# Projections of a transformer layer: SP's loads and VectorE's operations in source order, weight loads and splits by step, q statistics by pairs of tiles

## The chip, the core and the metric

The kernel runs on one core of a Trainium2 chip. The core has TensorE (PE, matmuls, with PEld for its weight loads), VectorE (DVE), ScalarE (ACT), GpSimd (POOL) and SyncE (SP, which here only issues DMAs). The metric is device time in microseconds of one execution; lower is better. Times of the kernel before are given as the median of three runs.

## The reference

One layer over 1,024 latent tokens of width 1,024 with 256 context tokens, all in float32. The part that matters here is the projection of the modulated input to queries, keys, values and gates:

```python
mod = jax.nn.silu(c) @ w_mod[l] + b_mod[l]            # 6 x 1024 modulation columns
h_c = ctx * (1.0 + mods_c[1]) + mods_c[0]             # context, modulated
kv_ctx = _context_kv(h_c, w_in[l], b_in[l], k_norm_g[l])
h = x * (1.0 + scale1) + shift1
proj = h @ w_in + b_in                                # q_a, k_a, v_a, q_b, k_b, v_b, gates
q_a = _rope_2d(heads(OFF_QA, OFF_KA, A_HEADS), rope)
q_b = _rope_2d(_qk_rms(heads(OFF_QB, OFF_KB, B_HEADS), q_norm_g), rope)
k_b = _rope_2d(_qk_rms(heads(OFF_KB, OFF_VB, B_KV_HEADS), k_norm_g), rope)
```

`_qk_rms` divides each head by the root of its mean square; `_rope_2d` is the axial rotation. After it come windowed attention (branch a, 8 heads) and global attention (branch b, 8 heads), the merge of both through sigmoid gates, a layer norm, a SwiGLU ConvFFN with 2,816 channels and a second layer norm. The output must be exact to float32's order, so each product is made of three matmuls.

## The kernel before

**Number format.** Every operand of a large product is split into a rounded high part and a low rest (`split`, line 81): ACT (or GpSimd) casts, and VectorE or GpSimd subtracts. `mm3` (line 90) issues high x high (L91), then the second operand's low part (L92), then the first operand's low part (L93).

**Order of the work.** The framework's planner orders each engine's instructions: it takes the program's order as priority and runs what it believes ready. Only from line 1192 on is PE's order that of the source. In the stage of this change, the projections, the planner orders all engines.

**Stages.** First the eight k steps of branch b's queries (`q1acc`, eight tiles of 128 tokens), each with its weights and two modulation columns. Their evacuation (`q_evac`, line 308) adds the bias. Then a list `order` (line 707) of groups runs: 3 gates, qa (tiles 0 to 3 of branch a's queries, eight k steps of 12 matmuls), 4 gates, qb (tiles 4 to 7, the same), 4 gates, ka (keys and values of tiles 0 to 4, eight k steps of 15), 1 gate, kb (tiles 5 to 7 and the two context tiles 8 and 9, steps of 15, six of them with context operands), 4 gates. A gate is one column tile of 128 channels in two halves of 512 tokens, 24 matmuls each.

**Weights.** `prefetch` (line 632) loads a weight into one of three `raw` buffers through SP's queue and splits it into `wp` buffers, eight in all, so four pairs. For gates GpSimd makes the low part (`wlg`), for q and kv weights VectorE (`wlqa`, `wlqb`, `wlka`, `wlkb`). For kb it also loads context (`cx`), modulates it on ACT and splits it on VectorE (`ch`, `cl`). The loop calls `prefetch` as far ahead as eight buffers allow: `ahead = [2 if gi in (0, 2, 3) else 4 for gi, _ in order]`, `while nxt < len(order) and sum(ahead[n:nxt + 1]) <= 8`.

**Modulation columns.** 48 columns (512 KB each) that are not needed at the start are handed out by `mods` (line 659), in proportion to the matmuls issued up to the last k step of ka. Each is a load on SP into a rotating 4 KB slot (`tmp`, from the list `hfree`) and one multiply-and-reduce on VectorE (L191).

**Side work.** `side_step` (line 696) runs one step of every post in flight and takes a new post from `queue`, each second time while `slow` is set. Posts are `qpost` (branch b: s1 with a folded rotation table on GpSimd and the statistics through `rms_scale`, s2 with the rotation; branch a: the rotation alone) and `kv_post` (s1: value split, statistics, rotation of branch a's key; s2: scaling, rotation and split of the keys; s3: four transposes on PE and copies). One rotation in three goes to GpSimd, the others to VectorE. The statistics of q square a tile on ACT into one half of `sqq`, reduce it on VectorE (L300), scale it there (L301), take the power on GpSimd (L302) and negate there (L337). At the last k step of ka and kb the sums are evacuated at once (L744) into one of two `kv` tiles. PSUM has eight banks, which accumulators, gates and transposes share.

Of the kernel before, what the change touches and what calls it, by code (L numbers as in the profile page):

```python
# [65 lines left out]
WARM = 5, 12  # L66
DNS = {u0 + 2 * n + (u0 == 20): (n, j0, j1) for u0, j0, j1 in ((16, 0, 4), (20, 4, 8), (24, 8, 11)) for n in range(3)}
# [3 lines left out]
def layer_kernel(  # L71
# [44 lines left out]
    mhalf = ctile([P, 8], F32, "mhalf")  # L116
# [179 lines left out]
    def rms_scale(x3, H, nm, sq, ss=None):  # L296
        nc.scalar.activation(sq.rearrange("p (h d) -> p h d", d=HD), x3, AF.Square)
        if ss is None:
            ss = ph1.tile([P, 8], F32, tag="ss", name=f"ss{nm}", bufs=4)[:, 0:H]
# [21 lines left out]
    def qpost(br, t):  # L321
# [36 lines left out]
    def kv_post(t, kv):  # L358
        st = {}
        kb = kv[:, 128:256].rearrange("p (h d) -> p h d", d=HD)  # L360

        def s1():
            vt = VT[t // 2][:, t % 2]
# [11 lines left out]
        def s2():  # L375
            rms_apply(kb, 2, st["ss"])
# [255 lines left out]
    def prefetch(gi, k):  # L632
        if gi == "g":
            hs = []
            for a in (0, 1):
                wr = raw(f"wg{k}_{a}")
                nc.sync.dma_start(wr.rearrange("p (a b) -> p a b", b=P), w_g[k][:, 4 * a:4 * a + 4])
                hs.append(wsplit(wr, f"g{k}_{a}", "gpsimd"))
            ready[gi, k] = hs
            return  # L640
        nm, src, tiles = groups[gi]
        wr = raw(f"w{nm}{k}")
        nc.sync.dma_start(wr, src[k])
# [109 lines left out]
    while queue or flight:  # L753
        side_step()
# [997 lines left out]
```

## Time and profile before

| what | value |
|---|---|
| median of 3 runs | 1588.32 us (1586.73 to 1589.17) |
| profiled execution | 1587.44 us |
| its span, first to last instruction | 1585.7 us |
| granted clock of PE, mean | 0.992 |
| PE busy | 1537.8 us (97%) |
| VectorE busy | 1195.1 us (75%) |
| ACT busy | 812.8 us (51%) |
| GpSimd busy | 753.0 us (47%) |

The projections behind branch b's queries take from about 55 to 344 us of the span. Busy time counts an instruction from its start to its end; matmuls overlap, each shown with some 0.39 us while the next starts 0.23 us after it, so PE's progress is best read from starts. A row of groups gives line, engine, operation, what is written from what, shapes and count, then busy us, mean ns of one, then idle time of the engine just before and what ended it. A row in order of time gives start and length in us and, in brackets, the idle time before and its releaser.

### The profile page before, as it was taken

What the parts mean: (1) busy time and instruction counts of PE and PEld (TensorE: products, weight loads), DVE (VectorE), ACT (ScalarE), POOL (GpSimd) and SP (SyncE); (2) the same over time, 40 slices, a digit from 0 to 9 for tenths busy, and PEclk for the clock granted to TensorE, in tenths of its full rate; (3) what the DMA queues carried; (4) which work ended last, traced back from release to release, by engine and by line L of the source; (5) the groups of instructions that cost most, each with busy time, mean ns of one, the idle gap of its engine ahead of it and who ended that gap; (6) DMA issues with size and microseconds to landing.
All of it is one profiled execution on the core that took longest, in us unless ns stands there. A gap on an engine that the chain in (4) does not pass through costs nothing.

```text
span 1585.7 us, 22137 instructions
## 1 busy us (share of the span) xinstructions
PE 1537.8 (97%) x7718; PEld 1275.6 (80%) x7718; DVE 1195.1 (75%) x1766; ACT 812.8 (51%) x1444; POOL 753.0 (47%) x731
## 2 busy tenths in 40 slices
PE   9999999999999999999999999999999999999996
PEld 7877788878886887777788898888888888888876
DVE  7897645628888777788674779888887887657886
ACT  5412222448888667788431565444444444435542
POOL 0673312416667556665423554666666674021132
PEclk9999999999999999999999999999999999999998
DMA  9785662322236555531451132333334446996721
GB/s 378 252 273 173 223 211 90 115 85 65 65 94 167 137 127 138 134 68 38 143 179 59 61 100 86 114 107 111 115 106 117 111 115 184 350 285 208 256 94 53
DMA packets 112225, 229.46 MB, mean 145 GB/s; under 512 B 12945, under 2 KB 27793, under 8 KB 112018
## 3 DMA queue, kind: packets, MB, share of 16 engines
q1 hardware_dynamic: 96816, 198.93, 37.9%
q0 software_dynamic: 10400, 20.19, 8.2%
q10 hardware_dynamic: 4898, 8.94, 1.5%
q8 instruction: 60, 0.98, 0.3%
q14 instruction: 51, 0.42, 0.1%
HBM read 176.83 MB, written 65.86 MB: 153 GB/s over the span
## 4 chain that ended last, share of the span: by engine, by line
PE 83%; DVE 6%; ACT 3%; issue 3%; DMA 2%; POOL 2%; ACTq 0%; SPq 0%; DVEq 0%; POOLq 0%
PE ptr L546 5%; PE p L92 4%; PE p L93 4%; PE p L91 4%; PE g L93 3%; PE g L91 3%; PE g L92 3%; PE b L93 3%; PE b L92 3%; PE b L91 3%; PE s L429 2%; PE av L567 2%; PE c L91 2%; PE d L93 2%; PE c L93 2%
## 5 line engine op out<-in xcount | busy, mean ns | idle before, releaser
L556 DVE TENSOR_TENSOR ptl<-ptr,pth 128x512 fp32r<-128x512 f32 x188 | 124.6, 684 | 27.9 <-ACT pth L555 25.6
L555 ACT CAST pth<-ptr 128x512 fp32r<-128x512 f32 x188 | 106.6, 588 | 56.6 <-PE ptr L546 32.8
L546 PE MATMUL ptr<-ident,p 128*128 128x128 f32 x816 | 126.8, 278 | 8.6 <-DVE ptl L556 6.6
L88 DVE TENSOR_TENSOR ld<-rd,hd 128x1024 fp32r<-128x1024 f32 x77 | 94.0, 1239 | 53.3 <-ACT hd L83 49.6
L441 ACT ACTIVATE p<-p,nm 128x1024 f32<-128x1024 f32 (+2 forms) x128 | 125.3, 981 | 10.6 <-DVE p L474 9.9
L546 PEld LDWEIGHTS ptr<-ident,p 128*128 128x128 f32 x816 | 93.7, 140 | 38.7 <-DVE ptl L556 12.5
L83 ACT CAST hd<-rd 128x1024 fp32r<-128x1024 f32 x77 | 79.2, 1050 | 80.4 <-PE p L93 47.1
L567 PE MATMUL av<-pth,VT 128*128 128x512 f32 x236 | 104.6, 443 | 1.0 <-ACT avs L573 0.5
L91 PE MATMUL p<-hd 128*128 128x512 f32 x264 | 103.2, 391 | 0.0
L93 PE MATMUL p<-hd,ld 128*128 128x512 f32 x264 | 102.7, 389 | 0.0
L92 PE MATMUL p<-ld,hd 128*128 128x512 f32 x264 | 102.7, 389 | 0.0
L93 PE MATMUL g<-hh,wlg 128*128 128x512 f32 x256 | 99.9, 390 | 0.9 <-POOL wlg L88 0.8
L91 PE MATMUL g<-hh,whg 128*128 128x512 f32 x256 | 100.0, 391 | 0.6 <-ACT whg L83 0.6
L88 POOL TENSOR_TENSOR wlg<-wg,whg 128x512 fp32r<-128x512 f32 x32 | 48.3, 1518 | 108.5 <-ACT whg L83 107.6
L92 PE MATMUL g<-hl,whg 128*128 128x512 f32 x256 | 99.6, 389 | 0.0
L568 PE MATMUL av<-ptl,VT 128*128 128x512 f32 x236 | 97.6, 414 | 2.0 <-POOL ptl L88 1.8
L474 DVE TENSOR_SCALAR_CACHE_REDUCE p<-s,cvt,nmc 128x1024 f32<-128x1024 f32 x64 | 84.4, 1339 | 12.3 <-PE s L430 12.0
L429 PE MATMUL s<-KL,q 128*128 128x512 f32 (+2 forms) x192 | 76.0, 396 | 3.8 <-ACT p_x L441 2.0
L191 DVE CUSTOM_DVE_ANT_0 wml<-wml,sc,bmc 128x1024 f32<-128x1024 f32 x32 | 44.5, 1399 | 39.3 <-DMA wml<-in_wmodT_dram 38.8
L85 POOL TENSOR_SCALAR pth<-prw 128x512 fp32r<-128x512 f32 x48 | 31.4, 653 | 86.1 <-ACT prw L552 62.0
L83 ACT CAST wS<-s 128x512 fp32r<-128x512 f32 x76 | 45.3, 621 | 51.8 <-POOL s L1094 51.0
L430 PE MATMUL s<-KL,q 128*128 128x512 f32 (+2 forms) x192 | 71.7, 373 | 0.0
(402 smaller groups left out, 4981.4 us busy)
## 6 DMA issues: line engine op xcount, KB each, us to landing
wml<-in_wmodT_dram SPq DMA_DIRECT2D x48, 512.0 KB
ru<-in_w_up_dram SPq DMA_DIRECT2D x38, 512.0 KB
rd<-td SPq DMA_DIRECT2D x55, 256.0 KB
rd<-sd SPq DMA_DIRECT2D x44, 256.0 KB
rd<-in_w_dn_dram SPq DMA_DIRECT2D x33, 256.0 KB
wm<-in_wmodT_dram SPq DMA_DIRECT2D x16, 512.0 KB
wg<-in_w_g_dram SPq DMA_DIRECT2D x32, 256.0 KB
sgd<-sg ACTq DMA_DIRECT2D x32, 256.0 KB
```

The lines of the kernel that those rows point to most:

```text
L83: nc.scalar.copy(hi, src)
L88: lo_eng.tensor_tensor(out=lo, in0=src, in1=hi.bitcast(F32), op=ALU.subtract)
L91: nc.tensor.matmul(ps, a[0], b[0], start=start, stop=False, skip_group_check=resumed)
L92: nc.tensor.matmul(ps, a[0], b[1], start=False, stop=False, skip_group_check=resumed)
L93: nc.tensor.matmul(ps, a[1], b[0], start=False, stop=stop, skip_group_check=resumed)
L429: nc.tensor.matmul(o, self.q[0][:, hs], ks, start=True, stop=False)
L441: nc.scalar.activation(p, s, AF.Exp, bias=nm[:, h:h + 1], scale=scale, accum_out=sm[:, h:h + 1])
L546: nc.tensor.transpose(tr[:, h * P:(h + 1) * P], self.pslice(h, n), ident)
L555: nc.scalar.copy(hi, tr)
L556: nc.vector.tensor_tensor(out=lo, in0=tr, in1=hi.bitcast(F32), op=ALU.subtract)
L567: nc.tensor.matmul(self.av, v, hi, start=first, stop=False)
L568: nc.tensor.matmul(self.av, v, lo, start=False, stop=self.left == 0)
```

## The change

1. The whole list runs in a region in which VectorE and SP issue in the source's order (`manual_schedule`); PE, ACT and GpSimd stay with the planner, and so does the place of the region's instructions among earlier and later ones of VectorE and SP.
2. The list is cut into steps (a gate half or a k step). At step n the load of step n+5 is issued (`WLOAD`), then the split of step n+3 (`WSPLIT`), then the context load of step n+2 and the context split of step n+1, for steps of both kv groups.
3. Columns are loaded four ahead (`MLOAD`); each `mods` call works on one that was loaded earlier and loads the next.
4. The statistics of q cover two tiles: one square of 128x1024, one reduction, one scale, one power, one negation. The squares of tiles 0 to 3 are issued among the evacuations, later ones right behind the reduction of four tiles before; `sqq` has two slots for it.
5. The evacuation of a kv tile moves from the end of its group into the post's s1.
6. Once all columns are done, a gate half is followed by two side steps.

```diff
-    def rms_scale(x3, H, nm, sq, ss=None):
+    def rms_scale(x3, H, nm, sq):
         nc.scalar.activation(sq.rearrange("p (h d) -> p h d", d=HD), x3, AF.Square)
-        if ss is None:
-            ss = ph1.tile([P, 8], F32, tag="ss", name=f"ss{nm}", bufs=4)[:, 0:H]
+        ss = ph1.tile([P, 8], F32, tag="ss", name=f"ss{nm}", bufs=4)[:, 0:H]
         nc.vector.tensor_reduce(out=ss, in_=sq.rearrange("p (h d) -> p h d", d=HD), axis=AX.X, op=ALU.add)
@@ -330,21 +332,37 @@
         def s1():
             st["tb"] = ph1.tile([P, 2, HD], F32, tag="tb", name=f"tbq{t}", bufs=4)
             gfold(st["tb"], 0, t, nc.gpsimd)
-            rms_scale(q3, 8, f"q{t}", sqq[0][:, t % 2], pqs[:, t])
-            if t == NT - 1:
-                sqq.clear()
-                hput("sqq")
-            nc.gpsimd.tensor_scalar(out=nqs[:, t], in0=pqs[:, t], scalar1=-1.0, scalar2=0.0, op0=ALU.mult, op1=ALU.add)
...
+            if t % 2 == 0:
+                qstats(t)
 
...
-    sqq = [ht("sqq", (P, 2, 512))]
+    sqq = [ht(f"sqq{n}", (P, 2, 512)) for n in (0, 1)]
+
+    def qsquare(t):
+        nc.scalar.activation(sqq[t // 2 % 2].rearrange("p a b -> p (a b)"), Q[1, t].rearrange("p a b -> p (a b)"),
+                             AF.Square)
+
+    def qstats(t):
+        sq = sqq[t // 2 % 2]
+        ss, ns = (a[:, t:t + 2].rearrange("p a b -> p (a b)") for a in (pqs, nqs))
+        nc.vector.tensor_reduce(out=ss, in_=sq.rearrange("p a (h d) -> p (a h) d", d=HD), axis=AX.X, op=ALU.add)
+        if t + 4 < NT:
+            qsquare(t + 4)
+        nc.vector.tensor_scalar(out=ss, in0=ss, scalar1=1.0 / HD, scalar2=QK_EPS, op0=ALU.mult, op1=ALU.add)
+        nc.gpsimd.tensor_tensor(out=ss, in0=ss, in1=mhalf, op=ALU.pow)
+        nc.gpsimd.tensor_scalar(out=ns, in0=ss, scalar1=-1.0, scalar2=0.0, op0=ALU.mult, op1=ALU.add)
+        if t + 2 == NT:
+            hput("sqq0", "sqq1")
+
     bias_qb = bias_tile(b_qb, "bias_qb")
     for t in range(NT):
         q_evac(1, t, acc[t], bias_qb)
+        if t in (1, 3):
+            qsquare(t - 1)
 
...
-    def kv_post(t, kv):
+    def kv_post(t, acc):
         st = {}
-        kb = kv[:, 128:256].rearrange("p (h d) -> p h d", d=HD)
 
         def s1():
+            kv = st["kv"] = ph1.tile([P, 512], F32, tag="kv", name=f"kv{t}", bufs=KVB)
+            nc.vector.tensor_tensor(out=kv, in0=acc, in1=bias_kv, op=ALU.add)
+            kb = st["kb"] = kv[:, 128:256].rearrange("p (h d) -> p h d", d=HD)
             vt = VT[t // 2][:, t % 2]
             v3 = kv[:, 256:512].rearrange("p (h d) -> p h d", d=HD)
             nc.scalar.copy(vt[:, :, 0:HD], v3)
...
-    def prefetch(gi, k):
+    def wload1(gi, k, a):
         if gi == "g":
-            hs = []
-            for a in (0, 1):
-                wr = raw(f"wg{k}_{a}")
-                nc.sync.dma_start(wr.rearrange("p (a b) -> p a b", b=P), w_g[k][:, 4 * a:4 * a + 4])
-                hs.append(wsplit(wr, f"g{k}_{a}", "gpsimd"))
-            ready[gi, k] = hs
-            return
-        nm, src, tiles = groups[gi]
-        wr = raw(f"w{nm}{k}")
-        nc.sync.dma_start(wr, src[k])
-        c = None
-        if NT in tiles:
-            cx = ph1.tile([P, NC], F32, tag="cx", name=f"cx{k}", bufs=2)
-            nc.sync.dma_start(cx, ctxT[k])
-            nc.scalar.activation(cx, cx, AF.Identity, bias=modx[:, k:k + 1], scale=modx[:, 8 + k:9 + k])
-            c = [ph1.tile([P, NC], R32, tag="ch", name=f"c{a}{k}", bufs=4) for a in "hl"]
-            split(cx, *c, nc.vector, nc.vector)
-        ready[gi, k] = wsplit(wr, f"{nm}{k}"), c
+            wr = raw(f"wg{k}_{a}")
+            nc.sync.dma_start(wr.rearrange("p (a b) -> p a b", b=P), w_g[k][:, 4 * a:4 * a + 4])
+        else:
+            wr = raw(f"w{groups[gi][0]}{k}")
+            nc.sync.dma_start(wr, groups[gi][1][k])
+        ready[gi, k, a, "raw"] = wr
+
+    def wpair(gi, k, a):
+        wr = ready.pop((gi, k, a, "raw"))
+        if gi == "g":
+            ready[gi, k, a] = wsplit(wr, f"g{k}_{a}", "gpsimd")
+        else:
+            ready[gi, k, a] = wsplit(wr, f"{groups[gi][0]}{k}")
+
+    def cload(gi, k):
+        cx = ready["cx", k] = ph1.tile([P, NC], F32, tag="cx", name=f"cx{k}", bufs=2)
+        nc.sync.dma_start(cx, ctxT[k])
+
+    def cpair(gi, k):
+        cx = ready.pop(("cx", k))
+        nc.scalar.activation(cx, cx, AF.Identity, bias=modx[:, k:k + 1], scale=modx[:, 8 + k:9 + k])
+        c = ready["c", k] = [ph1.tile([P, NC], R32, tag="ch", name=f"c{a}{k}", bufs=4) for a in "hl"]
+        split(cx, *c, nc.vector, nc.vector)
 
     late = [(col, scc, modx[:, col:col + 1]) for col in range(16)]
     late += [(col, sc, modc[:, col:col + 1]) for col in range(16, 48)]
 
     total = len(late)
     span = [0.0, 0.0]
+    coming = []
+
+    def mload():
+        col, row, o = late.pop(0)
+        w = tmp(f"wml{len(late)}")
+        nc.sync.dma_start(w, wmodT[col])
+        coming.append((col, row, o, w))
 
     def mods(us):
         span[0] += us
-        n = total - len(late)
-        for _ in range(min(int(total * span[0] / span[1] + 0.01) - n, len(late))):
-            col, row, o = late.pop(0)
-            w = tmp(f"wml{len(late)}")
-            nc.sync.dma_start(w, wmodT[col])
+        n = total - len(late) - len(coming)
+        for _ in range(min(int(total * span[0] / span[1] + 0.01) - n, total - n)):
+            col, row, o, w = coming.pop(0)
             mod(w, row, bmc[:, col:col + 1], o)
-            if not late:
+            if late:
+                mload()
+            elif not coming:
...
-        if late:
+        if late or coming:
             sg = ht(f"sg{f}_{hf}", (P, HALF))
             hput(f"sg{f}_{hf}")
...
-    ahead = [2 if gi in (0, 2, 3) else 4 for gi, _ in order]
     span[1] = sum(6 * KT if gi == "g" else 3 * len(groups[gi][2])
                   for gi, _ in order[:order.index((0, KT - 1)) + 1])
-    nxt = 0
-    for n, (gi, k) in enumerate(order):
-        while nxt < len(order) and sum(ahead[n:nxt + 1]) <= 8:
-            prefetch(*order[nxt])
-            nxt += 1
+    steps = [(gi, k, a) for gi, k in order for a in ((0, 1) if gi == "g" else (0,))]
+
+    def at(n, fn, *only):
+        if n < len(steps) and (not only or steps[n][0] in only):
+            gi, k, a = steps[n]
+            fn(*((gi, k) if only else (gi, k, a)))
+
+    inorder = ExitStack()
+    inorder.enter_context(tc.manual_schedule(engines={mybir.EngineType.DVE, mybir.EngineType.SP}))
+    for n in range(WLOAD):
+        at(n, wload1)
+        if n + WSPLIT - WLOAD >= 0:
+            at(n + WSPLIT - WLOAD, wpair)
+    for _ in range(MLOAD):
+        mload()
+    for n, (gi, k, a) in enumerate(steps):
+        at(n + WLOAD, wload1)
+        at(n + WSPLIT, wpair)
+        at(n + 2, cload, 0, 1)
+        at(n + 1, cpair, 0, 1)
         if gi == "g":
-            for hf in (0, 1):
-                last = gate(k, hf)
-                mods(3 * KT)
+            last = gate(k, a)
+            mods(3 * KT)
+            side_step()
+            if not (late or coming):
                 side_step()
             continue
         nm, src, tiles = groups[gi]
         if k == 0:
             acc = {t: acc_tile(f"acc{nm}{t}") for t in tiles}
             slow[0] = gi > 1
-        w, c = ready.pop((gi, k))
+        w = ready.pop((gi, k, 0))
+        c = ready.pop(("c", k), None)
         for t in tiles:
...
         mods(3 * len(tiles))
         if k == KT - 1:
             for t in tiles:
                 if gi < 2:
-                    kv = ph1.tile([P, 512], F32, tag="kv", name=f"kv{t}", bufs=KVB)
-                    nc.vector.tensor_tensor(out=kv, in0=acc[t], in1=bias_kv, op=ALU.add)
-                    queue.append(kv_post(t, kv))
+                    queue.append(kv_post(t, acc[t]))
                 else:
                     q_evac(0, t, acc[t], bias_qa)
                     queue.append(qpost(0, t))
@@ -750,6 +797,7 @@
                 queue += [[lambda u=u: units[u].qprep(acc_tile)] for u in (0, 1)]
         else:
             side_step()
+    inorder.close()
```

More of the change, by code (lines that the diff above doesn't have):

```diff
@@ L66 @@
 WARM = 5, 12
+WLOAD = 5
+WSPLIT = 3
+MLOAD = 4
 DNS = {u0 + 2 * n + (u0 == 20): (n, j0, j1) for u0, j0, j1 in ((16, 0, 4), (20, 4, 8), (24, 8, 11)) for n in range(3)}
@@ L115, in layer_kernel @@
     onesf = ctile([P, P], F32, "onesf")
-    mhalf = ctile([P, 8], F32, "mhalf")
+    mhalf = ctile([P, 16], F32, "mhalf")
     nc.vector.memset(onec, 1.0)
@@ L375, in s2 @@
         def s2():
+            kv, kb = st["kv"], st["kb"]
             rms_apply(kb, 2, st["ss"])
@@ L674, in gate @@
         for k in range(KT):
-            h, l = ready["g", f][k // 4]
+            h, l = ready["g", f, k // 4]
             n = slice(k % 4 * P, (k % 4 + 1) * P)
             mm3(ps, (h[:, n], l[:, n]), (hT[k][0][:, s], hT[k][1][:, s]), k == 0, k == KT - 1)
-        if late:
+        if late or coming:
             sg = ht(f"sg{f}_{hf}", (P, HALF))
@@ L733, in layer_kernel @@
                 s = slice(t * P, (t + 1) * P)
-                a = hT[k][0][:, s], hT[k][1][:, s]
+                x = hT[k][0][:, s], hT[k][1][:, s]
             else:
                 s = slice((t - NT) * P, (t - NT + 1) * P)
-                a = c[0][:, s], c[1][:, s]
-            mm3(acc[t], a, w, k == 0, k == KT - 1)
+                x = c[0][:, s], c[1][:, s]
+            mm3(acc[t], x, w, k == 0, k == KT - 1)
         mods(3 * len(tiles))
```

## The prediction

> **What bounds the kernel now.** I read the page first, then the stretch table, then the waits of PE, then the order of time of PE, ACT, DVE and SP around PE's longest wait.
>
> ```profile
> span 1585.7 us, 22137 instructions
> PE 1537.8 (97%) x7718; PEld 1275.6 (80%) x7718; DVE 1195.1 (75%) x1766; ACT 812.8 (51%) x1444; POOL 753.0 (47%) x731
> ```
>
> PE is the bound: it is without work for about 48 us in the whole span. A change to loads and to VectorE's order can win only what PE loses in the projections (55 to 344 us) and lose only what PE would newly wait there. So the question is where PE waits in that stage, and which wait the change would put there.
>
> ```profile
> PE accqa L92 <- DVE wlqa L88: 3.9, 1, 3.9
> PE accqb L92 <- DVE wlqb L88: 2.5, 2, 2.0
> PE g L93 <- POOL wlg L88: 0.8, 1, 0.8
> PE g L91 <- ACT whg L83: 0.6, 1, 0.6
> ```
>
> This is the whole answer of the waits for PE from 40 to 345 us (waiter, releaser, us in total, times, longest): every wait is for a split weight, and the large ones for the low half that VectorE makes (wlqa, wlqb). The order of time (start, length, instruction, idle before) gives their price; its first row is for later.
>
> ```profile
> 14.73 1.52 PE L93 MATMUL q1acc<-whqb,hl 128*128 128x512 f32 x6
> ...
> 92.62 0.39 PE L92 MATMUL accqa<-wlqa,hh 128*128 128x512 f32 x1
> ...
> 93.76 0.39 PE L91 MATMUL accqa<-whqa,hh 128*128 128x512 f32 x1
> 98.08 0.80 PE L92 MATMUL accqa<-wlqa,hh 128*128 128x512 f32 x1 [3.93 <-DVE wlqa L88]
> 98.67 0.63 PE L93 MATMUL accqa<-whqa,hl 128*128 128x512 f32 x1
> ...
> 102.94 0.47 PE L91 MATMUL accqa<-whqa,hh 128*128 128x512 f32 x1
> ...
> 176.91 0.39 PE L91 MATMUL accqb<-whqb,hh 128*128 128x512 f32 x1
> 179.33 0.50 PE L92 MATMUL accqb<-wlqb,hh 128*128 128x512 f32 x1 [2.03 <-DVE wlqb L88]
> 179.67 0.40 PE L93 MATMUL accqb<-whqb,hl 128*128 128x512 f32 x1
> 179.91 0.39 PE L91 MATMUL accqb<-whqb,hh 128*128 128x512 f32 x1
> ```
>
> Undisturbed matmuls start 0.228 us apart (five in 92.62 to 93.76). So the wait of L92 in accqa costs 98.08 - 93.76 - 0.23 = 4.1 us, and after it the eleven starts to 102.94 take 4.86 us where 2.5 would do: 2.4 us of slow clock. The wait at 179.33 costs 2.2 us, and nothing after it (starts 0.24 apart). The stretch table has the same (columns: length, then busy us of PE, PEld, DVE, ACT, POOL, granted clock, DMA share, GB/s):
>
> ```profile
> 90.00:100.00 10.00, 6.07 (x24) 4.64 (x23) 10.00 (x15) 2.87 (x5) 9.56 (x8) 0.81 0.81 280
> 100.00:110.00 10.00, 10.00 (x39) 8.11 (x38) 9.23 (x18) 1.86 (x3) 3.49 (x3) 0.84 0.87 294
> 170.00:180.00 10.00, 7.50 (x32) 5.57 (x31) 7.28 (x12) 1.86 (x3) 0.00 (x0) 1.00 0.71 271
> ```
>
> Why is wlqa late?
>
> ```profile
> 92.32 0.63 ACT L297 ACTIVATE sqq<-Q 128x512 f32<-128x512 f32 x1 [6.86 <-DVE cvt L300]
> 92.86 1.12 ACT L83 CAST whqa<-wqa 128x512 fp32r<-128x512 f32 x2
> ...
> 94.53 1.83 DVE L191 CUSTOM_DVE_ANT_0 wml<-wml,scc,bmc 128x1024 f32<-128x1024 f32 x1
> 96.29 1.73 DVE L88 TENSOR_TENSOR wlqa<-wqa,whqa 128x512 fp32r<-128x512 f32 x1
> ...
> 85.20 11.51 SPq L665 DMA_DIRECT2D wml<-in_wmodT_dram  x5
> 98.05 0.33 SPq L643 DMA_DIRECT2D wqa<-in_w_qa_dram  x1
> ```
>
> Three lines of work meet. ACT stood 6.9 us before a square of q, which waited for VectorE's reduction of an earlier one (L300) to free half of sqq; the casts of whqa were behind it. VectorE then took a modulation column (L191) before the low half. And SP was occupied from 85.2 to 96.7 with five column loads, so that the next weight load went out at 98.05.
>
> **The change, part by part.** *Order of SP and DVE.* Columns are now paced with the steps, 48 over 840 matmuls (0.69 per q step of 12, 1.37 per gate half of 24), loaded four ahead; a weight's load stands five steps ahead and its split three, ahead of the step's columns and side work. Eight wp buffers already allowed four pairs, so the depth of the split is what it was; new is that nothing of later steps gets in front. *Statistics.* The squares of tiles 0 to 3 come right behind the evacuations, the next ones behind a reduction of four tiles earlier, so ACT has no reason to stand as at 92.32. That takes away the wait and its cause: 4.1 + 2.4 + 2.2, and for the waits of 0.8, 0.6 and 2.5 - 2.0 us (each costs 0.16 more than it shows, 0.39 less 0.23, since a matmul's tail overlaps the next) 1.9 + 0.5 = 2.4. Sum of the gain: **11.1 us**, by these rows; at least 0 if the waits stay, and no more than this, since PE has no other wait there.
>
> Does VectorE keep up in line? Its prices:
>
> ```profile
> L191 DVE CUSTOM_DVE_ANT_0 wml<-wml,sc,bmc 128x1024 f32<-128x1024 f32 x32 | 44.5, 1399 | 39.3 <-DMA wml<-in_wmodT_dram 38.8 <-ACT sg L683 0.4
> L88 DVE TENSOR_TENSOR wlqb<-wqb,whqb 128x512 fp32r<-128x512 f32 x8 | 5.4, 687 | 4.2 <-ACT whqb L83 4.2
> L300 DVE TENSOR_REDUCE cvt<-sqq 128x8 f32<-128x512 f32 x8 | 5.4, 673 | 0.0
> L286 DVE TENSOR_TENSOR Q<-rt1q,rt2q 128x512 f32<-128x512 f32 x12 | 11.6, 968 | 0.0
> L284 DVE TENSOR_TENSOR rt2q<-Q,tbq 128x256 f32<-128x256 f32 x12 | 5.8, 513 | 0.0
> L278 DVE TENSOR_TENSOR rt1q<-Q,tbq 128x512 f32<-128x512 f32 x6 | 4.1, 679 | 0.0
> ```
>
> A q step lists 0.69 for the low half and 0.69 x 1.4 = 1.0 for columns: 1.7 us against 12 x 0.228 = 2.7 of PE. In qa come two rotations on VectorE (tiles 3 and 4, each 0.68 + 2 x 0.51 + 0.97 = 2.7) and one pair of statistics (twice 0.67, plus a scale: 1.6): 8 x 1.7 + 7.0 = 20.6 against 21.8. But it comes late into qa: both halves of a gate read both weight halves, so in the second half before qa the pair for the step three on gets its buffer only after 12 matmuls (2.7 us), and VectorE, in line, stands there before columns (1.9), a rotation and statistics (4.3): 2.7 + 1.3 + 6.2 = 10.2 against 5.4, 4.8 behind. Each plain step wins back 1.0, the fourth adds 3.3 and the sixth 1.7, so it is at most some 6 us behind; a split three steps ahead has 8.2 less 1.3 for cast and subtraction, 6.9. No wait by these prices (0), 3 us if GpSimd stretches three operations as it did L88 at 96.29 (1.73 against 0.69); nearer the first, I take **1.0**. In qb one rotation is left, and in gates GpSimd makes the low half. The four q evacuations at a group's end now hold VectorE until PE is through; behind them stand columns and side work of a gate half, for which nobody on PE waits.
>
> *Halved statistics* save VectorE about four reductions' fixed part and four scales, GpSimd four powers: off the path, 0. *Context splits for ka.* Step lists call cload and cpair for both kv groups, though only kb multiplies context: eight loads of 128 KB on SP, eight ACT operations and eight pairs of VectorE operations too many; in ka no side work is left (list: 0.7 + 0.8 + 0.86 x 1.4 = 2.7 of 3.4 us), so 0. *SP* now stands at a load whose buffer is not free, with all later loads behind it: a weight load has five steps (13.6 us in q), the longest such wait of before was 13.0:
>
> ```profile
> SPq L665 <- DVE modc L191: 40.4, 10, 13.0
> ```
>
> With eight or more rotating slots and four columns under way the slot's last user is finished, so 0; 2 us if one such wait stays.
>
> *The kv evacuations* move from ka's end into the side step, behind the split of kb1, and cpair is only one step ahead. Here lies the new wait.
>
> ```profile
> 255.00:281.00 26.00, 26.00 (x121) 21.53 (x120) 23.14 (x91) 7.38 (x19) 8.35 (x10) 1.00 0.28 83
> L87 DVE CAST ch<-cx 128x256 fp32r<-128x256 f32 x8 | 2.8, 355 | 3.8 <-PE acckb L92 3.8
> L88 DVE TENSOR_TENSOR cl<-cx,ch 128x256 fp32r<-128x256 f32 x8 | 3.7, 466 | 0.9 <-DVE ch L87 0.5
> L365 ACT CAST VT<-kv 128x256 fp32r<-128x256 f32 x10 | 4.1, 407 | 23.7 <-DVE kv L744 23.6
> L297 ACT ACTIVATE ktp<-kv 128x128 f32<-128x128 f32 x10 | 3.1, 307 | 0.0
> L683 ACT ACTIVATE sg<-g,bgc 128x512 f32<-128x512 f32 x32 | 21.8, 683 | 38.0 <-PE g L93 37.6 <-ACT sg L683 0.4
> ```
>
> In that stretch DVE did ka's five posts, five weight halves (3.5) and two context pairs (1.6): 18.0 / 5 = 3.6 us a post, say 1.9 in s1 and 1.7 in s2; in line s1 also waits for copy and square on ACT (0.41 + 0.31). From the end of ka (0): cast and half of kb1 (1.3) and two s1 (5.2) end at 6.5; kb2's half must wait for the middle of the second gate half and its cast (5.4 + 2.7 + 0.6), done at 9.4; then a context pair (0.8), two s2 (3.4), two s1 (5.2), kb3's half (0.7) and kb1's context pair (0.8): 20.3. PE reaches that operand after two gate halves (10.9), one kb step (3.4) and nine matmuls (2.0): 16.3. It would wait 4.0, and once more at kb2 (5.8 us further on the line against 1.4 + 2.0 on PE) 2.4; at kb3 the line has caught up. So 6.4 us if PE keeps strictly to the program's order; if the planner, which still orders PE, moves kb2's and kb3's nine matmuls ahead, 2.0 less each, 2.4; 0 if the line runs better than this. I take **2.4**. PSUM: kb needs five banks, two gate halves and two or three evacuated tiles free them by then; 0.
>
> *End of the stage.* Two side steps a gate half finish kb's posts four halves early, so the transposes that stand last on PE now go before:
>
> ```profile
> 343.96 0.45 PE L391 MATMUL ktr<-identr,ks 128*128 128x128 f32 x4
> 345.37 0.38 PE L429 MATMUL s<-KL,q 128*128 128x256 f32 x1 [0.96 <-ACT KC L396]
> ```
>
> Gain **0.9 us**. Sum: -11.1 + 1.0 + 2.4 - 0.9 = **-8.6 us**. The profiled execution took 1587.44 us (1.7 around its span), 0.9 under the median of 1588.32; so 1578.8 against it, and **1580** as a median.
>
> **A rule of the skill.** The rows: 3.93 us idle were followed by 4.9 us of starts 0.43 apart, 2.03 us idle by none. The Trainium skill, TensorE: Matmul & The Clock Gate, "What's actually happening", has the array fall to half clock after about 3.4 us without work and stay there for about 3.4 us; the rows agree in kind. By that page the slow stretch would have cost 1.7 us, an estimate, and the sum would be -7.9 us; I keep the row's 2.4. By the row at 98.08 a whole wait of 4.0 in kb would bring 2.4 us of slow clock too, against the change.
>
> **Rivals.**
> 1. *The line at kv.* If ACT is in the middle of a sigmoid (0.68) and a cast (half of the 1.12 above), each of five s1 waits some 1.3 us longer, and PE keeps to program order: 6.4 + 6.5 = 12.9, with 1.0 in qa against the gain of 12.0: 1590. For it: DVE was 23.14 of 26 us busy there. Against: the planner does put ready matmuls ahead on PE; at 14.73 six L93 stand together, because L91 and L92 of their tiles had gone first.
> 2. *It does not do what it says.* ACT's order is still the planner's; if a cast is put behind a copy that waits for VectorE (L365 waited 23.6 us in all), PE waits as before: 1588. Against: no square is now on a half buffer whose reduction is late.
> 3. *GpSimd stretches the line; slower.* While GpSimd was 9.56 of 10 us busy, L88 took 1.73 instead of 0.69 and L191 1.83 instead of 1.4. In line every stretch is handed on. With GpSimd busy throughout, a q step lists 1.73 + 0.69 x 1.83 = 3.0 and a rotation, doubled, about 5.5: qa 24 + 13 = 37 us against 21.8 and 6.9 of lead, 8 late; qb some 1; ka (1.7 + 1.6 + 1.6 against 3.4, lead 8) 4; kb's posts twice as long 10; two slow stretches 4.8. 28 - 12 = 16 more: 1604. It decides from some 15 us of new waits, which is GpSimd busy for over half of these steps. Against: its rotations are one tile in three, and in 170 to 180 us it had nothing at all. The Trainium skill, GPSIMD Engine Reference, "Key points", says that GpSimd shares its SBUF interfaces with VectorE and contends with its two-input instructions. By that rule, the row at 96.29 agrees.
>
> **How the numbers follow.** The forecast has 0.54, with 1575.5 (the gains of 12.0 and none of the new waits, rounded down) to 1585 (6.4 and 3 of new waits, and the slow clock once in part) as its own range; rival 1 0.14, rival 2 0.10, rival 3 0.18; 0.04 for later stages laid out differently by the planner, either way. Faster by over 0.2% (about what a measurement can tell from no change, 3.2 us): 0.54 + 0.03 of rival 1 + 0.02 = 0.59. Within: 0.11 + 0.10 = 0.21. Slower: 0.18 + 0.02 = 0.20. The range 1574 to 1592 holds all but rival 3.
>
> **What would show it.** Right: no PE wait for wlqa or wlqb, granted clock 1.00 from 90 to 110 us, no square on ACT that waits for L300 for microseconds, waits of 0 to 4 us before acckb's context matmuls, the attention's first score 8 to 10 us earlier. Wrong: waits for wl that moved to another step; VectorE standing before a column that has not landed; stretched L88 in qa; a later attention stage that is longer.

## The result: slower, by the spacing of matmuls that the change does not touch

The changed kernel takes 1600.24 us (median of 6 runs, 1599.71 to 1602.72) against 1588.74 for the kernel before on the same chip: a ratio of 1.0075, 95% interval [1.0062, 1.0088]. The prediction said 1580. Its profiled execution took 1599.71 us (before 1587.44). The head of its page:

```profile
span 1597.9 us, 22140 instructions
PE 1551.4 (97%) x7718; PEld 1273.3 (80%) x7718; DVE 1200.5 (75%) x1774; ACT 817.4 (51%) x1448; POOL 752.6 (47%) x723
```

PE has as many instructions as before and is busy 13.6 us longer (1537.8 before). So the loss is not a wait: the same matmuls take longer.

**The projections did what they were meant to do, up to ka.** The waits of PE in the changed kernel from 0 to 345 us:

```profile
PE ktr L412 <- DVE ks L91: 3.9, 3, 2.2
PE acckb L95 <- DVE wlkb L91: 2.3, 1, 2.3
PE cb L234 <- DVE mhalf L122: 1.1, 1, 1.1
PE g L96 <- POOL wlg L91: 0.4, 1, 0.4
```

The waits for wlqa and wlqb are gone; new are those for ks and wlkb, both in the stage of kb. The stretch table of the same stretches as before (columns as there):

```profile
90.00:100.00 10.00, 10.00 (x46) 8.29 (x45) 9.87 (x17) 3.12 (x5) 8.31 (x9) 1.00 0.53 182
100.00:110.00 10.00, 10.00 (x46) 8.29 (x45) 9.89 (x14) 2.08 (x4) 9.00 (x8) 1.00 0.64 220
170.00:180.00 10.00, 10.00 (x46) 8.29 (x45) 6.92 (x9) 1.87 (x3) 6.27 (x5) 1.00 0.77 262
255.00:281.00 26.00, 22.28 (x107) 16.66 (x105) 22.04 (x77) 10.61 (x34) 6.63 (x10) 1.00 0.25 70
```

There are 46 matmuls in ten microseconds in place of 24 and 39, and the clock is at 1.00. From 255 to 281 us there are 107 instead of 121, and PE stands for 3.7 us; because ka starts earlier, this stretch holds more of kb than it did before. Two marks in the order of time, ka's first matmul and the attention's first score, before:

```profile
230.92 0.39 PE L91 MATMUL accka<-whka,hh 128*128 128x512 f32 x1
345.37 0.38 PE L429 MATMUL s<-KL,q 128*128 128x256 f32 x1 [0.96 <-ACT KC L396]
```

and after:

```profile
219.15 0.39 PE L94 MATMUL accka<-whka,hh 128*128 128x512 f32 x1
340.87 0.28 PE L450 MATMUL s<-KL,q 128*128 128x256 f32 x1
```

ka starts 11.8 us earlier, the first score only 4.5: from ka to the score 7.3 us are lost. And the end comes 12.2 us later (span 1597.9 against 1585.7), so 16.7 us more are lost behind the score, in stages whose matmuls are the same.

**Where those 16.7 us are.** The stretch 1100 to 1200 us, in the middle of the up projection, before and then after:

```profile
1100.00:1200.00 100.00, 100.00 (x443) 82.84 (x442) 87.97 (x79) 49.62 (x69) 68.38 (x38) 1.00 0.36 106
```

```profile
1100.00:1200.00 100.00, 100.00 (x433) 80.90 (x432) 84.02 (x75) 47.86 (x68) 69.49 (x38) 1.00 0.36 109
```

PE is never idle in either, the granted clock is 1.00 in both, and ten matmuls fewer get through. The order of time shows how. Before:

```profile
1100.42 0.39 PE L93 MATMUL a<-B,wA 128*128 128x512 f32 x1
1100.65 0.39 PE L91 MATMUL a<-B,wA 128*128 128x512 f32 x1
...
1102.46 0.39 PE L93 MATMUL a<-B,wA 128*128 128x512 f32 x1
```

and after:

```profile
1100.16 0.40 PE L94 MATMUL d<-T24h,wA 128*128 128x512 f32 x1
1100.40 0.40 PE L95 MATMUL d<-T24l,wA 128*128 128x512 f32 x1
...
1102.48 0.40 PE L95 MATMUL a<-B,wA 128*128 128x512 f32 x1
```

Nine starts in 2.04 us before, 227 ns each; ten in 2.32 us after, 232 ns each. From the starts in whole nanoseconds that the trace keeps, twelve in a row:

```
before  227 226 227 227 226 227 227 226 227 227 226 227
after   233 236 224 234 228 230 235 233 230 236 228 230
```

Before, the spacing is a constant 226.7 ns; after, it wanders (from 224 to 236 in these twelve), with a mean of 232.0 from 1000 to 1400 us. The last long row (from 986 us) has 2380 such gaps, on average 5.16 ns longer (231.82 against 226.66): 12.3 us. The other 4.4 us come between the score and 986 us: 0.8 of them in the first hundred matmuls, the rest where 512-wide starts are on average 232.2 ns apart instead of 228.3 (500 to 985 us). In the changed kernel's projections, up to 240 us, the spacing is 226.7 as before.

### The profile page after: what moved, and what is told of

It is laid out like the page before. It is cut to its first block, busy times and chain, and to the rows that moved or that the text cites. A ratio compares the mean times of both kernels' runs of the same rounds, so it can differ in the third digit from the quotient of the medians.

```text
span 1597.9 us, 22140 instructions
## 1 busy us (share of the span) xinstructions
PE 1551.4 (97%) x7718; PEld 1273.3 (80%) x7718; DVE 1200.5 (75%) x1774; ACT 817.4 (51%) x1448; POOL 752.6 (47%) x723
## 4 chain that ended last, share of the span: by engine, by line
PE 83%; DVE 8%; ACT 4%; issue 2%; POOL 2%; DMA 0%; ACTq 0%; DVEq 0%; POOLq 0%
PE ptr L567 5%; PE p L96 4%; PE p L94 4%; PE p L95 4%; PE g L96 3%; PE g L94 3%; PE g L95 3%; PE b L96 3%; PE b L95 3%; PE b L94 3%; PE s L450 2%; PE d L94 2%; PE d L95 2%; PE c L94 2%; PE a L96 2%
## 5 line engine op out<-in xcount | busy, mean ns | idle before, releaser
L91 DVE TENSOR_TENSOR ld<-rd,hd 128x1024 fp32r<-128x1024 f32 x77 | 94.1, 1239 | 54.8 <-ACT hd L86 49.7
L91 POOL TENSOR_TENSOR wlg<-wg,whg 128x512 fp32r<-128x512 f32 x32 | 46.9, 1470 | 100.6 <-ACT whg L86 96.2
L86 ACT CAST wA<-ru 128x512 fp32r<-128x512 f32 x57 | 35.5, 622 | 68.6 <-PE d L96 38.3
```

Of the source, the lines that this page charges most:

```text
L86: nc.scalar.copy(hi, src)
L91: lo_eng.tensor_tensor(out=lo, in0=src, in1=hi.bitcast(F32), op=ALU.subtract)
```

## The experiments

**What the two programs do not share.** PE's matmuls behind the score have the same names, and the same order but for some 60 among the first 130. One constant is different: `mhalf` is 16 columns wide instead of 8, 32 bytes more, and it is allocated ahead of the large slots H0 to H18, so that all of these (KL, KC, VT, O, B, T13, T24 and others) stand 32 bytes higher; p, wA, hwb and the like are allocated from the other end of SBUF and stay. Then the tiles are dealt out to these slots in another order, some transposes go to another of their PSUM buffers, and PE has three event instructions more. Theories: **A**, the spacing depends on the addresses of a matmul's two operands to each other; **B**, it is the event instructions or the dealing out of tiles and buffers; **C**, a lasting state set where the projections end; **D**, the new order itself leads to it; **E**, only the one place is fast. The built program lists every tile's address; counts of "mixed" matmuls (operands whose addresses leave different remainders; the others are "matched") are worked out from that list. It has 7661 matmul instructions, of which 57 stand twice among the trace's 7718.

**The constant alone, in the kernel before (before_32b)**

```diff
-    mhalf = ctile([P, 8], F32, "mhalf")
+    mhalf = ctile([P, 16], F32, "mhalf")
```

> The kernel before with one number changed: the constant mhalf is 16 columns wide instead of 8, as in the changed kernel; it is read as before, and all else is as before. It is allocated ahead of the large slots (H0 to H18), so all of them move by 32 bytes. Theory A (the array's matmuls slow down when the two operands' byte addresses do not have the same remainder by 64): the share of such matmuls rises from 1180 to 4551 of 7661; starts of 128x512 matmuls from the b stage on go from 226.7 to about 232 ns, 2380 of them after 986 us alone cost 12.3 us, and those between the attention's start and there some 4.4: about 1605 us (1601 to 1606), with the projections unchanged (226.7 ns, attention's first score at 345.4). Theory B (the three more event instructions on PE, or another assignment of tiles to slots, both of which this kernel does not have): 1588.7, as before. Theory C (a lasting state set when the projections end in another way): 1588.7 too.

Measured: 1606.24 us, ratio 1.0111 [1.0096, 1.0125]. One number in the source, and the kernel before is at least as slow as the changed one. Its stretches:

```profile
200.00:240.00 40.00, 40.00 (x178) 33.13 (x177) 18.78 (x30) 9.38 (x15) 4.71 (x4) 1.00 0.65 217
1100.00:1200.00 100.00, 100.00 (x432) 80.86 (x432) 85.88 (x77) 46.70 (x66) 68.02 (x36) 1.00 0.34 107
```

The projections, whose operands hT and wp both stand at the unmoved end, go through at the full rate (178 in 40 us; 179 before), the later stage at the slow one. Theories B, C and D are not needed for it. (In this profile ka started 3.1 us later than before, at 234.00; that part of its time is not the spacing's. In the five profiles of programs that differ from the kernel before in addresses at most, it included, ka starts between 230.44 and 234.00.)

**64 bytes instead of 32 (after_64b, before_64b), and the identity too (after_all_same)**

```diff
+    ctile([P, 8], F32, "pad")                  # after_all_same alone, ahead of ident
-    mhalf = ctile([P, 16], F32, "mhalf")
+    mhalf = ctile([P, 24], F32, "mhalf")       # after_64b; before_64b the same from 8
```

> The changed kernel with mhalf 24 columns wide (the power reads the first 16): the slots stand 64 bytes, not 32, above those of the kernel before, so their remainder by 64 is that of before (1180 matmuls with mixed remainders, not 4551); all else is the changed kernel. Theory A: 226.7 ns from the b stage on, the whole loss after the first score (16.7 us: the score comes 4.5 us earlier and the end 12.2 later) goes, 1600.24 - 16.7 = 1583.5 (1582 to 1586). Theories B and C: 1600, nothing changes.

> Control: the kernel before with mhalf 24 columns wide, slots moved by 64 bytes. Theory A with 64 as the modulus: 1588.7, no change. If any move of the slots costs, or if the place counts by 128 bytes or more: up to 1605.

> The changed kernel (mhalf 16 wide) with an unused constant of 32 bytes ahead of the identity matrix: slots at the remainder 32 as before, and the identity too, so that only 84 of 7661 matmuls have operands of mixed remainders (1180 before: nearly all transposes of p and the masks). Theory A: as after_64b, and what the mixed transposes cost in the attention comes on top: 128x512 starts between 500 and 985 us were 229.8 and 227.9 apart before, which could go to 226.7 (456 x 3.1 + 763 x 1.2 = 2.3 us), and the transposes themselves may be nearer: 1580 (1577 to 1584). If the spacing in the attention comes from its waits alone: 1583.5. Theories B and C: 1600.

Measured: 1602.95 (1.0092), 1601.77 (1.0093) and 1601.65 us (1.0086). Theory A with 64 misses in all three; what came true is the other case of before_64b, that any move costs or that the place counts by 128 or more. (In after_64b the power reads the first 16 columns.) A move by 64 costs as much as one by 32, so the remainder by 64, which I had read off the two programs, is not what counts. The move itself still is: before_64b is the kernel before in all else, and has 433 matmuls from 1100 to 1200 us.

**Back to the old place, and 128 bytes (after_0b, before_128b)**

```diff
-    mhalf = ctile([P, 16], F32, "mhalf")
+    mhalf = ctile([P, 8], F32, "mhalf")                                        # after_0b
-        nc.gpsimd.tensor_tensor(out=ss, in0=ss, in1=mhalf, op=ALU.pow)
+        nc.gpsimd.tensor_tensor(out=pqs[:, t:t + 2], in0=pqs[:, t:t + 2],
+                                in1=mhalf.unsqueeze(1).to_broadcast([P, 2, 8]), op=ALU.pow)
```

before_128b is the kernel before with `mhalf` 40 wide.

> The changed kernel with mhalf 8 wide as before (the power of two tiles reads its 8 columns twice), so that the large slots stand where they stood before the change; the statistics, the order and all else are the changed kernel's. The shifts of 32 and 64 bytes both cost the kernel before 13 to 18 us, so the place counts by more than 64. Theory A (a matmul's spacing depends on whether its operands' addresses have the same remainder by 128 or more; by 128 there are 1256 mixed matmuls here, 4611 in the changed kernel): 226.7 ns from the b stage on, 1600.24 - 16.7 = 1583.5 (1582 to 1586). Theory D (the changed order itself leads to the slow spacing as well, in some way beside the place): 1600.

> The kernel before with mhalf 40 wide: the slots moved by 128 bytes. Theory A with the modulus 128 (1256 mixed matmuls, as before): 1588.6, and 226.7 ns. Theory A with the modulus 256 (4631 mixed, 1264 before): 1602 (1600 to 1606), some 232 ns. Theory E (only this one place of the slots is fast, whatever the modulus): 1602 too.

Measured: after_0b 1586.48 us, ratio 0.9988 [0.9974, 1.0002]; before_128b 1600.85, 1.0079 [1.0064, 1.0094]. With the slots at the old place the changed kernel is 14 us faster and PE is back at its old rate:

```profile
1100.00:1200.00 100.00, 100.00 (x443) 82.80 (x442) 88.14 (x79) 49.00 (x69) 68.49 (x38) 1.00 0.36 106
```

The order, the three event instructions and the dealing out of tiles and buffers are the changed kernel's (every slot stands 32 bytes lower, nothing else moves), so B, C and D are out, and A or E is left. 128 bytes are slow (x434), so a modulus would have to be 256 at least.

**Both ends by 32 bytes, and the slots by 256 (before_both32, before_m256)**

```diff
-    negsink = ctile([P, 8], F32, "negsink")                                    # before_both32
+    rconst = ctx.enter_context(tc.tile_pool(name="rconst", bufs=1, side="right"))
+    negsink = rconst.tile([P, 8], F32, tag="negsink", name="negsink")
-    bmc = ctile([P, 48], F32, "bmc")                                           # before_m256
-    bgc = ctile([P, 16], F32, "bgc")
+    bmc = ph1.tile([P, 48], F32, tag="bmc", name="bmc")
+    bgc = ph1.tile([P, 16], F32, tag="bgc", name="bgc")
...
```

> The kernel before with the constant negsink (32 bytes) taken from the left constants to a pool of its own at the right end of SBUF. Every slot on the left moves down by 32 bytes, and so does everything on the right: no operand stands where it stood, and all pairs of a matmul's operands have the same difference as before (1264 of 7661 mixed by 256, as before). Theory A (the two operands of a matmul, by 256): 1587.5 (1585 to 1590), 226.7 ns. Theory E (only this one place is fast): about 1601, 232 ns.

> The kernel before with the constants bmc and bgc (256 bytes) in the pool ph1 on the right: the large slots move down by 256 bytes, against the operands on the right. Theory A with the modulus 256 (1264 mixed, as before; by 512 it would be 4631): 1587.5 and 226.7 ns. Modulus 512 or more, or theory E: about 1601 and 232 ns.

Measured: 1587.29 us, 0.9992 [0.998, 1.0003], and 1588.54, 1.0005 [0.9994, 1.0017]. Theory E falls: in before_both32 every slot and every tile at the other end stands 32 bytes lower, and only the identity and the constants ahead of `negsink` stay. Both have 443 matmuls in the stretch; the row of before_both32:

```profile
1100.00:1200.00 100.00, 100.00 (x443) 82.79 (x442) 86.00 (x77) 48.63 (x68) 69.57 (x39) 1.00 0.38 113
```

All runs together (the mean start-to-start of 128x512 matmuls from 1000 to 1400 us, from the trace's nanoseconds; mixed by 256):

```
                slots against the other end   mixed of 7661    ns      ratio
before                      0                     1264       226.70
before_both32               0                     1264       226.70   0.9992
before_m256              -256                     1264       226.67   1.0005
after_0b                    0                     1264       226.68   0.9988
after, before_32b         +32                     4631       231.99   1.0075, 1.0111
after_64b, before_64b     +64                     4631       231.9    1.0092, 1.0093
after_all_same            +64                     4631       231.90   1.0086
before_128b              +128                     4631       231.17   1.0079
```

So a 128x512 matmul of this kernel starts 226.7 ns after the one before it when the operands of all matmuls around it are a multiple of 256 bytes apart, and some 232 ns when those of many are not. (By 512, 4159 are mixed in the kernel before, and it is fast.) Inside a program with many mixed ones the matched are hardly better: in the changed kernel's last long row 1056 matched matmuls are 231.2 ns from the next, 1326 mixed ones 232.5, and in the long row of before_64b it is the other way about, 232.4 and 232.1. So the runs show that the tiles of the two ends have to be in step by 256 bytes. They do not show that a matmul's own two operands are what counts, rather than those of its neighbours, and why the array behaves so is not shown either.

**How far it reaches (after_consts, kbfree1_ctx_ident)**

```diff
+    negsink = ctile([P, 8], F32, "negsink")
+    sinkb = ctile([P, 8], F32, "sinkb")
+    mhalf = ctile([P, 8], F32, "mhalf")
     ident = ctile([P, P], F32, "ident")
```

These three (in the second kernel `lnx` as well) are allocated ahead of the identity instead of behind it. The second kernel rests on after_kbfree1_ctx, below.

> As after_0b (mhalf 8 wide, slots where they stood before), and the three small constants negsink, sinkb and mhalf allocated ahead of the identity matrices instead of behind them: these move up by 96 bytes to the slots' remainder by 128. Mixed matmuls by 128: 92 of 7661 (1256 before, nearly all of them transposes of p with the identity). Theory A: after_0b's gain, and on top what the mixed transposes cost their neighbours in the attention: 512-wide starts between 500 and 985 us were 229.8 and 227.9 ns apart in the kernel before; at 226.7 they gain 456 x 3.1 + 763 x 1.2 ns = 2.3 us: 1581 (1577 to 1583.5). If the wider spacing in the attention comes from its waits alone: 1583.5, as after_0b.

> after_kbfree1_ctx with the constants negsink, sinkb, lnx and mhalf (224 bytes) allocated ahead of the identity matrices, so that the identity has the remainder of p by 256 (96); the slots stay. The 944 transposes of p, 128 columns each, then no longer mix: 308 mixed matmuls of 7661 instead of 1264. If theory A holds for short transposes and for the 512-wide matmuls between them, the attention gets faster: starts 229.7 ns apart between 500 and 985 us go towards 226.7, some 2 to 3 us in all, 1575.1 - 2.5 = 1572.6. If the spacing in the attention comes from its restarts after waits alone: 1575 (within 1.5).

Measured: 1586.04 us, 0.9988 [0.9977, 1.0], as after_0b; and 1575.88, 0.9919 [0.9904, 0.9933], as after_kbfree1_ctx. The first was laid out for a remainder by 128; by 256 the 944 transposes of p are still mixed in it (1036 of 7661 in all), so it tells nothing of them. The second has 308, with these transposes matched, and they cost nothing that shows: between 500 and 810 us the 512-wide starts are 228.9 ns apart in it, and 229.1 in after_kbfree1_ctx, where they are mixed. That the wider spacing there comes from restarts after waits is likely but was not tried by itself.

**What ka to the score loses (after_ctx, after_kbfree, after_kbfree1, after_kbfree1_ctx)**

With the place mended, the change still gives 1586.48, not 1580. All four rest on after_0b:

```diff
+            if gi == 0:                          # after_kbfree, after_kbfree1, _ctx
+                inorder.close()                  # ahead of ka's kv posts
...
             side_step()                          # after_kbfree1, after_kbfree1_ctx
-            if not (late or coming):
-                side_step()
...
+    for n, (gi, k, a) in enumerate(steps):       # after_ctx, after_kbfree1_ctx
+        if gi == 1:
+            ctxl.setdefault(n - (4 if k < 2 else 2), []).append((gi, k))
+            ctxp.setdefault(n - (3 if k < 2 else 1), []).append((gi, k))
...
-        at(n + 2, cload, 0, 1)
-        at(n + 1, cpair, 0, 1)
+        for m in ctxl.get(n, ()):
+            cload(*m)
+        for m in ctxp.get(n, ()):
+            cpair(*m)
```

> As after_0b, with the context's loads and splits for kb alone (ka's eight useless ones are gone) and for kb0 and kb1 two steps earlier (load four, split three steps ahead). If part of the 5.9 us that the changed kernel loses in the gate between ka and kb and in kb comes from context splits in VectorE's line: 1 to 2.5 us less than after_0b, with the wait for wlkb (2.3 us) gone. If the line is the five kv posts alone: the same as after_0b.

> As after_0b, but VectorE and SP go back to the planner's order at ka's end (the order in source ends ahead of ka's kv posts instead of at the stage's end). after_0b starts ka 11.3 us earlier than the kernel before and the attention's first score only 2.7 earlier, so 8.6 us go in the gate, kb and the last gates. If the line of VectorE there is the cause: they come back, in whole or in large part: 1586.5 - 8.6 = 1578 (1577 to 1581). If it is something else in the change (two side steps a gate half, the evacuation in the post, the useless context splits): 1585 to 1587.

> As after_kbfree, and one side step a gate half again instead of two once the columns are done. If the second side step brings the last transposes forward, as the prediction had it (0.9 us): 1579 against 1578. If it only puts more posts in front of the splits of kb: 1 to 3 us better than after_kbfree.

> after_kbfree1 with the context's loads and splits for kb alone, and kb0's and kb1's two steps earlier, as in after_ctx. after_kbfree1 still loses 3.0 us before kb0's first context matmul (a wait for ch of 2.8) and some 1.7 us of half clock behind it (nine starts 0.43 apart). If the context split stands too late in VectorE's order: both go, 1581.6 - 4.5 = 1577 (1576 to 1579). If VectorE is simply behind there: 1581.5, with another wait in its place.

Measured, with the two marks from the order of time (before: 230.92 and 345.37, 114.45 apart):

```
                      us       ratio                    ka      score    apart
after_0b            1586.48   0.9988 [0.9974, 1.0002]  219.59  342.62   123.03
after_ctx           1585.42   0.9987 [0.9976, 0.9998]  219.88  342.97   123.09
after_kbfree        1583.71   0.9972 [0.9961, 0.9983]  219.78  339.51   119.73
after_kbfree1       1581.62   0.9958 [0.9945, 0.9972]  219.59  338.87   119.28
after_kbfree1_ctx   1575.07   0.9921 [0.9908, 0.9933]  219.04  333.50   114.46
```

(The 8.6 us of after_0b hold 1.3 more than the changed kernel's 7.3: from 315 to 325 us its granted clock is 0.83 with 34 matmuls, against 1.00 and 40.) VectorE's line is one part of the cause. In after_0b VectorE stands ten times before the reduction of a k square (L302), behind ACT, with the splits for kb behind it; the row of it in the waits of DVE from 240 to 345 us:

```profile
DVE ssk L302 <- ACT ktp L300: 9.2, 10, 2.2
```

One post of the line, in DVE's order of time in the same kernel:

```profile
263.97 0.69 DVE L382 TENSOR_TENSOR kv<-accka,bias_kv 128x512 f32<-128x512 f32 x1
265.60 0.28 DVE L302 TENSOR_REDUCE ssk<-ktp 128x2 f32<-128x128 f32 x1 [0.94 <-ACT ktp L300]
...
267.25 0.68 DVE L91 TENSOR_TENSOR wlkb<-wkb,whkb 128x512 fp32r<-128x512 f32 x1
```

From the evacuation to the half of the next weight 3.3 us pass, one post's first part. The planner's order (after_kbfree) takes 3.3 of the 8.6 us out. Without the second side step the score comes 0.6 us earlier and the 200 matmuls behind it take 32.2 us instead of 33.1 (32.2 before); the median is 2.1 lower, though the intervals still overlap. So the transposes that it brings forward were no gain. What was left in after_kbfree1 was one wait, for the context pair:

```profile
266.68 0.39 PE L96 MATMUL acckb<-whkb,hl 128*128 128x512 f32 x1
269.87 0.50 PE L94 MATMUL acckb<-whkb,ch 128*128 128x512 f32 x1 [2.80 <-DVE ch L90]
...
270.87 0.63 PE L94 MATMUL acckb<-whkb,ch 128*128 128x512 f32 x1
271.30 0.63 PE L95 MATMUL acckb<-wlkb,ch 128*128 128x512 f32 x1
```

With the pair two steps earlier it is gone, with its slow clock; ka to the score is as long as before (114.46), the whole gain of the projections reaches the end, and this is a version that beats both kernels: 1575.07 us. (The edit also drops ka's eight useless context splits; which of the two did it was not separated.) The same edit in the line of source order (after_ctx) moved no mark: PE's waits for ks fell from 3.9 to 2.6 us, the 2.3 for wlkb stayed, and 1.6 for ch came.

**Statistics or order (before_stats)**: the kernel before with `sqq0`, `sqq1`, `qsquare` and `qstats` alone, `mhalf` 8 wide.

> The kernel before with the q statistics two tiles at a time alone (mhalf 8 wide, its columns read twice; slots in place; orders the planner's). The kernel with everything reaches ka 11.3 us earlier. If the chain of square and reduction is what made the weight split late (the square that stood 6.9 us on ACT): the wait of 4.1 and its slow clock of 2.4 go, ka starts some 6.5 us earlier and the whole takes 1581. If the columns in front of the split on VectorE and SP are the cause: ka starts as before (within 1.5 us), 1587.

Measured: 1590.42 us, 1.0026 [1.0014, 1.0038], slower. The waits of PE:

```profile
PE accqb L92 <- DVE wlqb L88: 7.5, 3, 4.3
PE accqa L92 <- DVE wlqa L88: 2.5, 2, 1.5
```

Without the order the waits for the low halves stay, 10.0 us in all against 6.4 before, most of them now in qb. ka starts at 235.49, 4.6 us later than before and later than in any of the five profiles with the orders of before (230.44 to 234.00).

## Why the prediction was wrong, step by step

- **Where it failed: halved statistics, "off the path, 0".** I counted the operations and not the constant that serves them. `mhalf` grew by 32 bytes and pushed every large slot out of step with the operands at the other end: before_32b, the one edit alone, is 1.0111; after_0b, the change without it, 0.9988. After that the later stages were no longer those of before, which the sum took for granted; of all cases only the 0.04 for "later stages laid out differently" came near, and it named the planner, which was not it.
- **The gain of 11.1 less 1.0: right, slightly small.** ka starts 11.8 us earlier; no wait for wlqa or wlqb, clock 1.00 from 90 to 110 us. VectorE's lag in qa cost nothing; the 1.0 was too much. But the 4.1 and 2.4 for the one long wait in qa were read off one execution: in before_64b, which differs from the kernel before in addresses alone, the longest wait for wlqa is 1.6 us and the clock stays at 1.00 from 90 to 100 us, the two waits in gates are 1.8 and 1.3 us, and ka still starts at 230.44.
- **Its cause: half right.** "That takes away the wait and its cause" gave the statistics a share. By before_stats they alone give none; it takes the order. Whether the order alone gives all of it was not run.
- **The kv line: the mechanism right, the size wrong.** Waits in kb for what VectorE makes, behind the posts: seen (2.3 for wlkb, 3.9 for ks). The term was 2.4, with 0.9 to be won at the end of the stage: 1.5 of loss in all. Measured 7.3 in the changed kernel, 8.6 in after_0b. A post's first part took 3.3 us up to the next split instead of 2.6 (rival 1 had 1.3 more a post, which was too much), and I had PE wait for splits alone; the transposes of ks, which PE has between gates, wait for the same line.
- **The end of the stage: wrong sign.** Two side steps a gate half were to gain 0.9; without the second the score comes 0.6 us earlier (after_kbfree1 against after_kbfree).
- **Context splits for ka, 0: no loss seen** while the line stands (after_ctx against after_0b: the ranges of 1585.42 and 1586.48 overlap). But that edit, with kb's first pairs earlier, is worth some 6 us once the line is gone (6.5 by the medians, 5.9 by the ratios), 4.8 of them ahead of the score.
- **SP in order, 0: no loss seen.** PE waits for no load in the stage.
- **Rival 3 came near the number (1604) with a mechanism that did not happen:** L91 in qa took 0.68 to 0.82 us a piece around 95 us with GpSimd 8.31 and 9.00 of 10 us busy, and no wait came of it.
- **The clock.** The row of before had 3.93 us idle followed by half clock and 2.03 by none. In after_kbfree1 2.80 us idle are followed by starts 0.43 apart (granted clock 0.91 from 260 to 280 us). The Trainium skill, TensorE: Matmul & The Clock Gate, "What's actually happening", gives about 3.4 us without work. These runs show the half clock after less, and not each time: a wait of 2.19 us for ks near 319 us goes with 0.83 from 315 to 325 us in after_0b, and one of 2.19 us at the same place with 1.00 in the changed kernel.

With the place mended (after_0b) the sum at the score is -11.3 + 8.6 = -2.7 us, and the ratio leaves about 2 us of gain at the end, in an interval that still holds none.

## What to carry to other kernels

Read what a change does to the allocation: a constant of 32 bytes can move every tile behind it. Keep the tiles that long rows of matmuls read a multiple of 256 bytes apart (in this kernel 0.8 to 1.1% hung on it), and when PE is never idle at granted clock 1.00 and gets fewer matmuls through, look at addresses before looking at instructions. Here an order by hand was a gain where the line was mostly splits, and a loss where a waiting post stood in it: end it there.

## What the runs showed of the hardware

The start-to-start of 128x512 float32r matmuls has two values at granted clock 1.00: 226.7 ns, all but a few gaps 226 or 227, and about 232 (231.2 to 232.0) wandering between 224 and 241. In every run here it was the first when the tiles at the two ends of SBUF stood to each other as in the kernel before or were moved against each other by 256 bytes, and the second when they were moved by 32, 64 or 128. Narrow ones do not follow: 256-wide starts between 500 and 986 us were 119.7 ns apart before and 118.4 in the changed kernel. I had expected addresses in SBUF to cost nothing.
